# Grouped attention scores as full-array products over stacked query halves, with the convolution branch moved last

## The chip, the cores and the metric

One core of one Trainium2 chip runs the whole program. The metric is the device time of one execution in microseconds (us); the kernel before takes 743.72 us in the median of three runs (743.72 to 745.99).

## What is computed

The reference is a two-layer decoder trunk for 256 tokens of width 1024, in float32. Each layer mixes three branches that read one input projection, and then runs a gated feed-forward network with a short convolution:

```
h = rms_norm(x, attn_norm[l])
parts = split(h @ w_in[l])            # 13 parts
y_a = conv_module(...)                # 256 channels: 31 taps, layer norm, silu, 256x256 product
y_b = nsa_mixer(...)                  # 8 heads of 64 in 2 groups: compressed, selected, window attention
y_c = dilated_mixer(...)              # 3 dilations x 4 heads of 64
x = x + concat([y_a, y_b, y_c]) @ w_out[l]
x = x + conv_ffn(rms_norm(x, ffn_norm[l]), ...)   # up to 2 x 2816, 3 taps, silu * value, down
```

In `nsa_mixer` a head's query meets three sets of keys: its group's selected keys (256 tokens; with this sequence every block is selected), its window keys (256) and 15 compressed keys (padded to 16). Each set has its own softmax, and the three results are added with a gate each.

## The kernel before

Tokens lie in two tiles of 128 (`t`). Every dense product is made exact enough from two float32r halves of each operand: the weights come from memory as float32 (`raw`), ScalarE copies them to `whi` (L212) and VectorE subtracts to get `wlo` (L215), and `dense3` (L453 to L456) issues three products, hi by hi, hi by lo and lo by hi. Weights are consumed in one fixed stream of pieces, and `take` lets conversion run three pieces ahead.

The mixing stage of a layer runs from the chunks `a0`/`a` (keys, values, gates), `b` (queries of the grouped attention), `c0`/`c1` (convolution input) through a list of steps, `ORDER`: `np(i)` scores, softmax and transposes of head pair i of the grouped attention (`nsa_pair`), `nf(g)` its compressed branch and the products with the values (`nsa_finish`), `dq`, `dk`, `dv` dilated projections, `da`, `ds`, `pv` dilated attention, `t(n)` n taps of the convolution on VectorE, `ct` the convolution's tail (`conv_tail`: layer norm, silu, 256x256 product). Then `proj("out", ...)` sums eight pieces of 128 input rows, in `OUT_ORDER` (0 and 1 are the convolution's channels, 2 to 5 the grouped heads, 6 and 7 the dilated pairs): the first four pieces by piece, the last four (`TAIL`) for each quarter of the output. The steps are written in this order, and a planner orders each engine's instructions by the order written, their dependencies and costs that it assumes, so that work of neighbouring steps interleaves; each engine then runs its own list in order.

Grouped scores: q is turned (L703) into `QT`, 128 rows for a pair of heads, head j in rows 64j to 64j+63. `KG[g]` holds the keys of a group twice, in both row halves, as [window tile 1 ... compressed ... selected], 528 columns. A pair has three groups of scores: one for token tile 0 (L742, 272 columns: one key tile of each set and the compressed keys) and two for tile 1 (L756, 256 and 272 columns). In each group a float32 product for head 0 uses rows 0 to 63 of the array and one for head 1 rows 64 to 127; each stands in the trace as two matmul records. The scores lie in one PSUM tile of two banks (`sc_bank`, one buffer); VectorE adds the masks and takes the row minimum (L746, L759), ScalarE takes the exponential (L767, L771) and multiplies by the inverse sums (copies with a scale, L212 `ms<-ms,dd`), the array turns them (L783, L789), and L819 and L822 multiply with the values, head j into rows 64j of the PSUM tile `o`.

Compressed branch: `cs` is turned into `pc`, 64 rows, and one float32 product with 64 contraction rows (L823) adds both heads of a pair through `vbig`.

The end: `proj("down", ...)` sums 22 pieces into two single-bank tiles (`da`, token tile 0) and the two banks of one tile `db` (token tile 1). After all of them four adds to x are written, and in the last layer four stores.

PSUM tiles: `mm` three banks, `tp` two, `sc` two as one tile, `o` one. `conv_tail` uses `o` four times, and the out projection's last quarter uses `o` too.

Of the kernel before, what the change touches and what calls it, by code (L numbers as in the profile page):

```python
# [44 lines left out]
OUT_ORDER = (2, 3, 4, 5, 6, 0, 1, 7)  # L45
# [118 lines left out]
ORDER = "np(0) dq(0) t(6) np(1) dk(0) t(6) nf(0) np(2) dv(0) t(6) np(3) nf(1) da(0) dq(1) t(10) dk(1) t(100) ds(1) dv(1) ct(0) pv(1)"  # L164
# [26 lines left out]
def tile_hybrid_trunk(ctx, tc, x_in, pos_in, stream, feats, gains, norms, const_in, out):  # L191
# [261 lines left out]
    def dense3(o, a_hi, a_lo, b_hi, b_lo, start, stop):  # L453
        nc.tensor.matmul(o, a_hi, b_hi, start=start, stop=False)  # L454
        nc.tensor.matmul(o, a_hi, b_lo, start=False, stop=False)  # L455
        nc.tensor.matmul(o, a_lo, b_hi, start=False, stop=stop)  # L456
# [50 lines left out]
    for l in range(L):  # L507
# [87 lines left out]
        state["w1"] = lambda h: mp.tile([P, 3, 3, P], F32, tag="pT", name=f"w1{h}", bufs=4).rearrange("p a b c -> p (a b c)")[:, :PIECE]  # L595
# [4 lines left out]
        KG = [mp.tile([P, 528], F32, name=f"KG{g}") for g in range(2)]  # L600
# [3 lines left out]
        vbig = mp.tile([64, 2, 4, 64], F32, name="vbig")  # L604
# [7 lines left out]
        def section_a(split):  # L612
# [12 lines left out]
            for t in range(NT):  # L625
                kr = krs[t]
                tp = tp_bank(f"tpk{t}")
                for i in range(4):
                    nc.tensor.transpose(tp[:, i * P:(i + 1) * P], kr[:, i * P:(i + 1) * P], ident)
                for g in range(2):  # L630
                    copy_act(KG[g][:, P - t * P:2 * P - t * P], tp[:, g * P:(g + 1) * P])
                    copy_act(KG[g][:, 272 + t * P:272 + t * P + P], tp[:, (2 + g) * P:(3 + g) * P])

        def section_a0(split):
# [46 lines left out]
            for g in range(2):  # L681
                tt(vbig[:, g], cp2[0:64, 64 + g * 64:128 + g * 64].unsqueeze(1).broadcast_to([64, 4, 64]),
# [3 lines left out]
            for g in range(2):  # L686
                copy_act(KG[g][:, 256:272], tpq[:, g * 16:g * 16 + 16])

# [8 lines left out]
        QT = mp.tile([P, 4, S], F32, tag="QT", name="QT", bufs=1)  # L697
        banks = tok_chunk("b", 512, False, f"B{l}")
        qrs = rope(banks, 8, 0, (0, 1), "q")
        for t in range(NT):  # L700
            tp = tp_bank(f"tpq{t}")
            for i in range(4):
                nc.tensor.transpose(tp[:, i * P:(i + 1) * P], qrs[t][:, i * P:(i + 1) * P], ident)  # L703
            copy_act(QT[:, :, t * P:(t + 1) * P], tp.rearrange("p (k c) -> p k c", k=4))
# [10 lines left out]
        ts(dwh, dw, 0.5, None, ALU.mult)  # L715
# [14 lines left out]
        def nsa_pair(pair):  # L730
# [9 lines left out]
                for j in range(2):  # L740
                    hp_ = slice(j * 64, j * 64 + 64)
# [339 lines left out]
```

## Time and profile before

| | |
|---|---|
| median of 3 runs | 743.72 us |
| the profiled execution | 750.38 us, of it span 748.6 us |
| TensorE matmul (PE) busy | 729.1 us (97%) |
| VectorE (DVE) busy | 593.9 us (79%) |
| ScalarE (ACT) busy | 485.3 us (65%) |
| GpSimd (POOL) busy | 25.4 us (3%) |
| granted TensorE clock, mean | 0.993 |

A row of a timeline gives start, duration, engine, line, operation, what it writes and reads, shapes, and how many instructions are merged into it. Matmul durations include the way through the array, so consecutive ones overlap; what one costs is the distance from its start to the next start. A group's row gives count, busy time together, mean of one, and the idle time before it. "128*64" on a matmul means 128 contraction rows and 64 output rows of the array.

### The profile page before, as it was taken

To read this page: it belongs to the slowest core of one execution; us is meant where nothing else is said; L and a number is where in the kernel's file an instruction comes from. 1 tells how busy PE (TensorE), PEld (TensorE's weight loads), DVE (VectorE), ACT (ScalarE), POOL (GpSimd) and SP (SyncE) were. 2 spreads that over 40 slices of the span, in tenths; PEclk is the share of its full clock that TensorE was granted. 3 is DMA by queue.
4 is the path that set the end of the run, shared out by engine and by line. 5 is a ranking of instruction groups with operands and counts; after the bars stand their busy time and mean duration, and the time that the engine had idled before them with its cause. 6 is when DMAs were issued, how large, how long until landed. Compare 5 with 4: busy or idle time off the path is not lost.

```text
span 748.6 us, 13381 instructions
## 1 busy us (share of the span) xinstructions
PE 729.1 (97%) x4794; PEld 639.7 (85%) x4794; DVE 593.9 (79%) x1363; ACT 485.3 (65%) x1168; POOL 25.4 (3%) x67
## 2 busy tenths in 40 slices
PE   7899999999999999999999999999999999999997
PEld 5779777887899999988868887779779999999885
DVE  7689999986888888864487599999868988988441
ACT  5667999665577666653357579997546767676330
POOL 5200000000000000000040000000000000000000
PEclk9799999999999999999999999999999999999999
DMA  8654223453375665566538232236344666666631
GB/s 312 218 171 125 85 86 106 133 171 119 123 245 181 191 188 185 182 212 197 177 116 276 84 119 65 85 102 180 112 136 170 198 200 194 195 199 195 199 114 57
DMA packets 36005, 119.84 MB, mean 160 GB/s; under 512 B 4113, under 2 KB 4385, under 8 KB 35938
## 3 DMA queue, kind: packets, MB, share of 16 engines
q1 hardware_dynamic: 35714, 118.70, 50.1%
q8 instruction: 38, 0.62, 0.3%
q0 software_dynamic: 224, 0.28, 0.2%
q14 instruction: 29, 0.24, 0.1%
HBM read 117.91 MB, written 1.05 MB: 159 GB/s over the span
## 4 chain that ended last, share of the span: by engine, by line
PE 84%; DVE 7%; ACT 6%; issue 2%; DMA 1%; SPq 0%; DVEq 0%; ACTq 0%
PE up L455 10%; PE up L456 10%; PE up L454 10%; PE da L455 3%; PE da L454 3%; PE da L456 3%; PE db L454 2%; PE db L455 2%; PE db L456 2%; DVE wlo L215 2%; ACT whi L212 2%; PE hid L662 1%; PE sc L756 1%; PE Dk L454 1%; PE Dk L456 1%
## 5 line engine op out<-in xcount | busy, mean ns | idle before, releaser
L215 DVE TENSOR_TENSOR wlo<-raw,whi 128x1024 fp32r<-128x1024 f32 (+3 forms) x232 | 259.4, 1124 | 85.7 <-ACT whi L212 84.6
L212 ACT ACTIVATE whi<-raw 128x1024 fp32r<-128x1024 f32 (+3 forms) x232 | 224.6, 979 | 101.4 <-PE db L456 53.6
L454 PE MATMUL up<-xT_hi,whi 128*128 128x256 f32 x640 | 178.4, 279 | 0.0
L455 PE MATMUL up<-xT_lo,whi 128*128 128x256 f32 x640 | 178.2, 279 | 0.0
L456 PE MATMUL up<-xT_hi,wlo 128*128 128x256 f32 x640 | 178.2, 279 | 0.0
L455 PEld LDWEIGHTS up<-xT_lo,whi 128*128 128x128 f32 x640 | 121.5, 190 | 0.0
L454 PEld LDWEIGHTS up<-xT_hi,whi 128*128 128x128 f32 x640 | 120.1, 188 | 0.0
L456 PEld LDWEIGHTS up<-xT_hi,wlo 128*128 128x128 f32 x640 | 120.1, 188 | 0.0
L225 DVE SCALAR_TENSOR_TENSOR u<-up,ffeat,u 128x255 f32<-128x255 f32 (+1 forms) x176 | 80.0, 478 | 2.6
L225 DVE SCALAR_TENSOR_TENSOR acc<-a_pad,dwh,acc 128x256 f32<-128x256 f32 x120 | 53.6, 479 | 0.3 <-ACT acc L720 0.2
L1034 ACT ACTIVATE sl<-u 128x256 f32<-128x256 f32 x44 | 18.1, 416 | 48.7 <-DVE u L225 48.6
L1027 ACT ACTIVATE u<-up,ffeat 128x256 f32<-128x256 f32 x88 | 44.1, 551 | 0.0
L454 PE MATMUL da<-whi,gT_hi 128*128 128x512 f32 x88 | 34.3, 389 | 0.0
L455 PE MATMUL da<-wlo,gT_hi 128*128 128x512 f32 x88 | 34.3, 389 | 0.0
L456 PE MATMUL db<-whi,gT_lo 128*128 128x512 f32 x88 | 34.2, 389 | 0.0
L456 PE MATMUL da<-whi,gT_lo 128*128 128x512 f32 x88 | 34.2, 389 | 0.0
L454 PE MATMUL db<-whi,gT_hi 128*128 128x512 f32 x88 | 34.2, 389 | 0.0
L455 PE MATMUL db<-wlo,gT_hi 128*128 128x512 f32 x88 | 34.2, 389 | 0.0
L454 PE MATMUL A<-whi,xT_hi 128*128 128x280 f32 (+1 forms) x64 | 23.9, 373 | 0.4 <-ACT xT_hi L212 0.4
L212 ACT ACTIVATE ms<-ms,dd 128x128 f32<-128x128 f32 (+1 forms) x64 | 24.2, 448 | 0.0
L456 PE MATMUL A<-whi,xT_lo 128*128 128x280 f32 (+1 forms) x64 | 23.7, 372 | 0.4 <-DVE xT_lo L215 0.4
L455 PE MATMUL A<-wlo,xT_hi 128*128 128x280 f32 (+1 forms) x64 | 23.0, 363 | 0.0
(342 smaller groups left out, 1564.4 us busy)
## 6 DMA issues: line engine op xcount, KB each, us to landing
raw<-in_stream SPq DMA_DIRECT2D x172, 512.0 KB, 4.1
raw<-in_stream SPq DMA_DIRECT2D x48, 384.0 KB, 3.1
raw<-in_stream SPq DMA_DIRECT2D x8, 280.0 KB, 5.0
w<-in_stream SPq DMA_DIRECT2D x4, 512.0 KB, 6.1
gain<-in_norms SPq DMA_DIRECT2D x3, 512.0 KB, 3.5
x<-in_x SPq DMA_DIRECT2D x4, 256.0 KB, 4.3
out<-x SPq DMA_DIRECT2D x4, 256.0 KB, 2.1
feat<-in_feats SPq DMA_DIRECT2D x2, 339.0 KB, 5.1
```

Of the source, the lines that this page charges most:

```text
L212: return nc.scalar.activation(out=o, in_=i, func=AF.Copy, **kw)
L215: return nc.vector.tensor_tensor(out=o, in0=a, in1=b, op=op)
L225: return nc.vector.scalar_tensor_tensor(out=o, in0=a, scalar=s, in1=b, op0=op0, op1=op1)
L454: nc.tensor.matmul(o, a_hi, b_hi, start=start, stop=False)
L455: nc.tensor.matmul(o, a_hi, b_lo, start=False, stop=False)
L456: nc.tensor.matmul(o, a_lo, b_hi, start=False, stop=stop)
L662: nc.tensor.matmul(hp[:, 0:64], w1[i // 8][:, i % 8, :], flat[:, i].rearrange("p a h c -> p (a h c)"), start=(i == 0), stop=(i == 15))
L756: nc.tensor.matmul(sc[:, j * 512:j * 512 + n], QT[hp_, pair, P:2 * P], keys[hp_], start=True, stop=True)
L1027: nc.scalar.activation(out=u[:, h], in_=z, func=AF.Identity, scale=c[:, 2:3], bias=c[:, 3:4])
L1034: nc.scalar.activation(out=sl_, in_=u[:, 0], func=AF.Silu)
```

## The change

Keys and queries of the grouped attention are split into float32r halves. `zq` holds for each head the 64 high parts and the 64 low parts of q next to each other, so that one turn of 128 columns stacks them in the contraction rows (`QS`, 8 heads instead of 4 pairs: 16 turns a layer for 8). `KH` and `KL` take the place of `KG`; each score is the sum of two float32r products with all 128 rows, one with `KH` and one with `KL`. The scaling of the larger scores (128x256, 16 a layer) goes from ScalarE to VectorE. `pc` and `vbig` get 64 rows of zeros (GpSimd), and the compressed product becomes two with 128 contraction rows and 64 output rows. Fewer taps stand in the early steps, 16 of the 60 after `dv(1)`; `ct` comes after `pv(1)`, and the convolution's two pieces come last in the out projection, whose last quarter accumulates in `sc` instead of `o`. In the last layer the adds to x and the stores are written between the products of the down projection's tail, and the last quarter is made in two halves of 256 columns. The half of the taps' weights (`dwh`) is made on GpSimd. `pT` buffers shrink from nine blocks of 128 to eight.

```diff
-OUT_ORDER = (2, 3, 4, 5, 6, 0, 1, 7)
+OUT_ORDER = (2, 3, 4, 5, 6, 7, 0, 1)
...
-ORDER = "np(0) dq(0) t(6) np(1) dk(0) t(6) nf(0) np(2) dv(0) t(6) np(3) nf(1) da(0) dq(1) t(10) dk(1) t(100) ds(1) dv(1) ct(0) pv(1)"
+ORDER = "np(0) dq(0) t(3) np(1) dk(0) t(3) nf(0) np(2) dv(0) t(6) np(3) nf(1) da(0) dq(1) t(12) dk(1) t(20) ds(1) dv(1) t(100) pv(1) ct(0)"
...
-        KG = [mp.tile([P, 528], F32, name=f"KG{g}") for g in range(2)]
+        KH = mp.tile([P, 2, 528], F32R, name="KH")
+        KL = mp.tile([P, 2, 528], F32R, name="KL")
+
+        def split_keys(cols, src):
+            copy_act(KH[:, :, cols], src)
+            tt(KL[:, :, cols], src, KH[:, :, cols].bitcast(F32), ALU.subtract)
+
...
-        vbig = mp.tile([64, 2, 4, 64], F32, name="vbig")
+        vbig = sp.tile([P, D], F32, tag="xn", name=f"vbig{l}", bufs=1)[:, 0:512].rearrange("p (g r d) -> p g r d", g=2, r=4)
+        nc.gpsimd.memset(vbig[64:P], 0.0)
...
-                for g in range(2):
-                    copy_act(KG[g][:, P - t * P:2 * P - t * P], tp[:, g * P:(g + 1) * P])
-                    copy_act(KG[g][:, 272 + t * P:272 + t * P + P], tp[:, (2 + g) * P:(3 + g) * P])
+                tv = tp.rearrange("p (w g c) -> p w g c", w=2, g=2)
+                split_keys(slice(P - t * P, 2 * P - t * P), tv[:, 0])
+                split_keys(slice(272 + t * P, 272 + t * P + P), tv[:, 1])
...
-        QT = mp.tile([P, 4, S], F32, tag="QT", name="QT", bufs=1)
+        QS = mp.tile([P, 8, S], F32R, tag="QT", name="QS", bufs=1)
...
         for t in range(NT):
-            tp = tp_bank(f"tpq{t}")
-            for i in range(4):
-                nc.tensor.transpose(tp[:, i * P:(i + 1) * P], qrs[t][:, i * P:(i + 1) * P], ident)
-            copy_act(QT[:, :, t * P:(t + 1) * P], tp.rearrange("p (k c) -> p k c", k=4))
+            z = qrs[t].rearrange("p (h d) -> p h d", h=8)
+            zq = mp.tile([P, 8, P], F32, tag="pT", name=f"zq{t}", bufs=4).rearrange("p b c -> p (b c)")[:, 0:1024].bitcast(F32R)
+            zq = zq.rearrange("p (h u d) -> p h u d", h=8, u=2)
+            copy_act(zq[:, :, 0], z)
+            tt(zq[:, :, 1], z, zq[:, :, 0].bitcast(F32), ALU.subtract)
+            for half in range(2):
+                tp = tp_bank(f"tpq{t}{half}")
+                for i in range(4):
+                    nc.tensor.transpose(tp[:, i * P:(i + 1) * P], zq[:, half * 4 + i].rearrange("p u d -> p (u d)").bitcast(F32), ident)
+                copy_act(QS[:, half * 4:half * 4 + 4, t * P:(t + 1) * P], tp.rearrange("p (k c) -> p k c", k=4))
...
-        ts(dwh, dw, 0.5, None, ALU.mult)
+        ts(dwh, dw, 0.5, 1.0, ALU.mult, ALU.mult, eng=nc.gpsimd)
...
-                    hp_ = slice(j * 64, j * 64 + 64)
-                    nc.tensor.matmul(sc[:, j * 512:j * 512 + 272], QT[hp_, pair, 0:P], KG[g][hp_, P:P + 272], start=True, stop=True)
+                    for u, keys in enumerate((KH, KL)):
+                        nc.tensor.matmul(sc[:, j * 512:j * 512 + 272], QS[:, 2 * pair + j, 0:P], keys[:, g, P:P + 272], start=u == 0, stop=u == 1)
...
-                        hp_ = slice(j * 64, j * 64 + 64)
-                        nc.tensor.matmul(sc[:, j * 512:j * 512 + n], QT[hp_, pair, P:2 * P], keys[hp_], start=True, stop=True)
+                        for u, keys in enumerate((KH, KL)):
+                            nc.tensor.matmul(sc[:, j * 512:j * 512 + n], QS[:, 2 * pair + j, P:2 * P], keys[:, g, 256 * w:256 * w + n],
+                                             start=u == 0, stop=u == 1)
...
-                        copy_act(msl[j][:, w], msl[j][:, w], scale=dd[:, 1, j, w:w + 1])
+                        ts(msl[j][:, w], msl[j][:, w], dd[:, 1, j, w:w + 1], None, ALU.mult)
...
-            pc = mp.tile([P, S], F32, tag="cth", name=f"pc{g}", bufs=1)[0:64]
-            copy_act(pc, tp[0:64, 0:S])
+            pc = mp.tile([P, S], F32, tag="cth", name=f"pc{g}", bufs=1)
+            nc.gpsimd.memset(pc[64:P], 0.0)
+            copy_act(pc[0:64], tp[0:64, 0:S])
...
-                nc.tensor.matmul(ob[:, 0:S], vbig[:, g, 2 * pr:2 * pr + 2].rearrange("p a d -> p (a d)"), pc, start=False, stop=True, skip_group_check=True)
+                for j in range(2):
+                    nc.tensor.matmul(ob[j * 64:j * 64 + 64, 0:S], vbig[:, g, 2 * pr + j], pc, start=False, stop=True, skip_group_check=True)
...
-        def proj(name, npieces, kts, a_hi, a_lo, acc, tail):
-            def run(t, w, i, nhs=(0, 1)):
+        def proj(name, npieces, kts, a_hi, a_lo, acc, tail, done=None):
+            def run(t, w, i, nhs=(0, 1), part=None):
...
+                    c0, c1 = part or (0, 512)
+                    sl = slice(nh * 512 + c0, nh * 512 + c1)
+                    dense3(acc[t][nh][:, c0:c1], a_hi[:, kk, t * P:(t + 1) * P], a_lo[:, kk, t * P:(t + 1) * P], hi[:, sl], lo[:, sl],
+                           i == 0, i == npieces - 1, skip_group_check=done is not None and t == NT - 1 and nh == 1)
...
-                    for i in range(tail):
-                        run(t, ws[i], npieces - tail + i, (nh,))
+                    last = done is not None and t == NT - 1 and nh == 1
+                    for part in ((0, 256), (256, 512)) if last else ((0, 512),):
+                        for i in range(tail):
+                            run(t, ws[i], npieces - tail + i, (nh,), part)
+                        if done is not None:
+                            done(t, nh, part)
...
-        obs = [[mm_bank(f"oa{l}{i}") for i in range(2)], [mm_bank(f"ob{l}0"), o_bank(f"ob{l}1")]]
+        obs = [[mm_bank(f"oa{l}{i}") for i in range(2)], [mm_bank(f"ob{l}0"), sc_bank(f"ob{l}1")[:, 0:512]]]
...
+        dacc = [dnb, [scb[:, 0:512], scb[:, 512:1024]]]
+
+        def residual(t, nh, part):
+            sl = slice(nh * 512 + part[0], nh * 512 + part[1])
+            tt(x_sb[t][:, sl], x_sb[t][:, sl], dacc[t][nh][:, part[0]:part[1]], ALU.add)
+            if l == L - 1:
+                nc.sync.dma_start(out[0, t * P:(t + 1) * P, sl], x_sb[t][:, sl])
+
+        proj("down", NF, list(range(NF)), gT_hi, gT_lo, dacc, 4, residual if l == L - 1 else None)
```

## Rows read from the trace of the kernel before

**Rows 1.** The page, part 1: busy time, share, instructions of each engine.
```profile
PE 729.1 (97%) x4794; PEld 639.7 (85%) x4794; DVE 593.9 (79%) x1363; ACT 485.3 (65%) x1168; POOL 25.4 (3%) x67
```
**Rows 2.** By stretch: length, then busy PE, PEld, DVE, ACT, POOL, clock, DMA.
```profile
40.00:187.00 147.00, 145.70 (x892) 118.90 (x891) 130.71 (x399) 111.57 (x372) 0.00 (x0) 1.00 0.39 124
165.00:187.00 22.00, 21.84 (x132) 17.05 (x130) 15.37 (x32) 12.72 (x24) 0.00 (x0) 1.00 0.30 98
400.00:560.00 160.00, 156.77 (x966) 128.12 (x965) 134.79 (x412) 118.40 (x380) 0.00 (x0) 1.00 0.40 123
```
**Rows 3.** Timeline of PE from 467 to 472 us, around two groups of scores.
```profile
467.56 0.70 PE L756 MATMUL sc<-KG,QT 64*128 64x256 f32 x2
468.18 0.44 PE L789 MATMUL tp<-ident,ms 128*128 128x128 f32 x2
...
470.16 0.34 PE L455 MATMUL Dv<-wlo,xT_hi 128*128 128x384 f32 x1
470.33 0.33 PE L454 MATMUL Dv<-whi,xT_hi 128*128 128x384 f32 x1
470.59 0.73 PE L756 MATMUL sc<-KG,QT 64*128 64x272 f32 x4
471.25 0.45 PE L455 MATMUL Dv<-wlo,xT_hi 128*128 128x384 f32 x1
471.54 0.34 PE L456 MATMUL Dv<-whi,xT_lo 128*128 128x384 f32 x1
```
**Rows 4.** Timeline of PE near 20 us: dense float32r products of 280 columns.
```profile
19.98 0.29 PE L454 MATMUL A<-whi,xT_hi 128*128 128x280 f32 x1
20.11 0.29 PE L455 MATMUL A<-wlo,xT_hi 128*128 128x280 f32 x1
```
**Rows 5.** Timeline of PE near 484 us: values, compressed product, turns.
```profile
484.14 0.60 PE L819 MATMUL o<-pT,vN 128*64 128x256 f32 x4
484.57 0.39 PE L822 MATMUL o<-pT,vN 128*64 128x128 f32 x4
484.89 0.70 PE L823 MATMUL o<-pc,vbig 64*128 64x256 f32 x2
485.51 0.44 PE L789 MATMUL tp<-ident,ms 128*128 128x128 f32 x2
```
**Rows 6.** Timeline of PE near 441 us: the turns of q.
```profile
441.48 0.63 PE L703 MATMUL tpq<-ident,z1q 128*128 128x128 f32 x4 [0.71 <-DVE z1q L215]
441.86 0.42 PE L456 MATMUL Dq<-whi,xT_lo 128*128 128x384 f32 x1
```
**Rows 7.** Groups of DVE instructions from 60 to 190 us.
```profile
L225 DVE SCALAR_TENSOR_TENSOR acc<-a_pad,dwh,acc 128x256 f32<-128x256 f32 x60 | 26.8, 479 | 0.0
...
L220 DVE TENSOR_SCALAR dm<-dm,ddd 128x512 f32<-128x512 f32 x8 | 3.5, 481 | 0.0
...
L215 DVE TENSOR_TENSOR yT_lo<-o,yT_hi 128x256 fp32r<-128x256 f32 x4 | 1.7, 421 | 0.4 <-ACT yT_hi L212 0.4
...
L215 DVE TENSOR_TENSOR z1q<-z1q,rrq 128x512 f32<-128x512 f32 x2 | 1.3, 685 | 0.0
```
**Rows 8.** Groups of ACT instructions from 60 to 190 us.
```profile
L212 ACT ACTIVATE ms<-ms,dd 128x256 f32<-128x256 f32 x16 | 7.3, 502 | 0.0
```
**Rows 9.** Timeline of DVE: first and last step of the convolution's tail, layer 0.
```profile
158.81 0.41 DVE L215 TENSOR_TENSOR acc<-acc,lnm 128x256 f32<-128x256 f32 x1
...
175.24 0.43 DVE L215 TENSOR_TENSOR yT_lo<-acc,yT_hi 128x256 fp32r<-128x256 f32 x1 [0.92 <-ACT yT_hi L212]
```
**Rows 10.** The chain that ended last: the out projection's last add in layer 0.
```profile
192.39 0.68 DVE x L215
```
**Rows 11.** Timeline of the end, from 743 us.
```profile
743.16 0.39 PE L455 MATMUL db<-wlo,gT_hi 128*128 128x512 f32 x1
...
743.39 0.39 PE L456 MATMUL db<-whi,gT_lo 128*128 128x512 f32 x1
743.82 1.28 DVE L215 TENSOR_TENSOR x<-x,db 128x512 f32<-128x512 f32 x2 [4.75 <-PE db L456]
```

## What I expect and why

> **What bounds the kernel.** I read the page's busy times first, then busy time by stretch, then the timeline of PE, then groups of DVE and ACT. PE is busy 97% of the span, DVE 79%, ACT 65% [rows 1]. A busy PE need not be a full one, so the stretches count: in both mixing stages PE is busy 98 to 99%, at a granted clock of 1.00, the 2.4 GHz level [rows 2]. In the timeline the next matmul of a dense run starts 0.17 us after the last (384 columns) with nothing between [rows 3]. So PE's list of instructions sets the time, and what the change saves or adds is first the sum of starts-to-starts on PE. DVE comes second, and close: it is busy 130.7 of 147 us (89%) in the mixing stage of layer 0, 134.8 of 160 (84%) in layer 1 [rows 2]. That is the room in which DVE may take on work while PE's stage shrinks.
>
> **Part 1, scores.** From the code: 4 pairs, 3 groups each, 2 layers are 24 groups, each with two float32 products of two records. In the trace they come in two patterns. Where both heads stand next to each other (19 groups), the dense product before starts at 470.33 and would be followed 0.17 later; the group starts 0.09 after that, takes 0.66 to the next start, and that next dense product takes 0.29 instead of 0.17 [rows 3]: 0.09 + 0.66 + 0.12 = 0.87 us. Where other instructions came between the heads (5 groups), one head alone takes 0.62 [rows 3]; with the same 0.09 on entry, 1.42 us for two. Old sum: 19 x 0.87 + 5 x 1.42 = 23.6 us. The new group has four float32r products in the full array, the shape of the dense ones. The nearest row, 280 columns, has 0.13 us from start to start [rows 4]; by columns 0.126 for 272 and 0.119 for 256. New sum: 16 groups x 4 x 0.126 + 8 x 4 x 0.119 = 11.9 us. Saved: 11.7 us. Bounds: at the 0.17 of the 384-column products [rows 3] the new sum is 16.3 and 7.3 are saved; 12.5 if entry to the split groups cost more than I counted.
>
> The Trainium skill, TensorEngine Tiling (Array Packing), "Key Properties", says that a change of tiling mode drains the array; by that the 0.09 and 0.12 at the borders are part of the price and go, as I count them. The Trainium skill, TensorEngine Tiling (Array Packing), "When to Use Tiling", speaks against the change: a contraction of 64 should be packed two to the array. The trace agrees that packing works (0.66 for two heads, 0.62 for one); what the rule would make of the time is a rival below.
>
> **Part 2, turns of q.** Eight more a layer. Four take 0.38 us from the first to the next dense start [rows 6]: 16 x 0.095 = 1.5 us, I take 1.6. The step before them now also has an ACT copy and a DVE subtraction of 128x512 (0.69 each by the nearest DVE row) [rows 7]; PE already waited 0.71 us there for the rotated q [rows 6], and I charge the longer chain below, in what PE doesn't realise; its bounds are nothing, if dense work of `dq` is moved in front, and 1.4 us a layer.
>
> **Part 3, compressed products.** One now takes 0.62 us plus 0.10 on entry: the four 128-column records before it, two at a time side by side, would be through at 484.79, and it starts at 484.89 [rows 5]. The new one has the shape of the product with the values, whose four records of 256 columns take 0.43 us [rows 5], with no change of shape before it and the 0.10 then on exit. 8 x (0.72 - 0.53) = 1.5 us saved; bounds zero (heads not side by side) and 2.3 (no exit).
>
> **PE together:** 11.7 + 1.5 - 1.6 = 11.6 us less, 5.8 a layer.
>
> **Part 4, what DVE takes on.** Per layer: 16 scalings of 128x256. The nearest row is the same operation on 128x512, 0.481 us [rows 7]; half is 0.24, the 128x256 subtraction from PSUM, 0.42, is the upper end; I take 0.27, nearer to the same operation, 4.3 us (3.8 to 6.7). Low parts of the keys: four of 128x256 from PSUM at 0.42 and one small, 1.9 us. Low parts of q: two of 128x512 at 0.685 [rows 7], 1.4 us. Together 7.6 us (7.1 to 10.0). `dwh` on GpSimd takes a little off DVE, and GpSimd is busy 25 us in all [rows 1]; the two clears of zeros wait in its queue for the buffers of `xn` and `cth`, and behind the first stand the rotation tables in layer 1, which I cost at nothing as long as the planner doesn't put the clear ahead of them; if it does, some 2 us. ACT loses 16 x 0.50 = 8 us a layer [rows 8] and gains four copies of q.
>
> Layer 0: 130.7 + 7.6 = 138.3 us of DVE in 147 - 5.8 = 141.2 us, 98%. Layer 1: 134.8 + 7.6 = 142.4 in 154.2, 92%. In layer 0 that is more than DVE can hold while its operands come from PE and ACT. At 95% the stretch takes 145.6 us and saves 1.4, at 97% 142.6 and 4.4; I take 3. In layer 1 I take 5 of 5.8, the rest going to the longer q chain. Realised: 8 us of 11.6.
>
> **Part 5, taps later, convolution last.** The early steps lose 6 taps, 6 x 0.45 = 2.7 us of DVE (26.8 us for 60) [rows 7] where scores wait for row minima, and 16 taps, 7.2 us, come after `dv(1)`, where DVE is at 15.4 of 22 us [rows 2]. I cost the move at nothing, covered by out-projection pieces that don't need the convolution: its tail ended at 175.7 [rows 9], the last add of the out projection came at 192.4 [rows 10], so PE had some 16 us of work behind it; 2 of 8 pieces (24 matmuls of 0.23 [rows 11], 5.5 us) need it and 5.8 are saved, which leaves 5 us by which it may slip. Without that cover it is the rival that is slower.
>
> **Part 6, the end.** Both adds to the last token tile ran after the last matmul, 1.28 us together [rows 11], though the first one's operands were complete 12 matmuls earlier: reads of one bank of the two-bank tile waited for the other. With the last quarter halved, one add of 128x256 (0.42) [rows 7] remains: 0.86 us saved at best. But a wait of that kind also works the other way: PE's next product into the tile, with the rest of the list behind it, waits for the add that was written before it. After the first quarter: 0.43 to the add's start, 0.69 for the add, less the 0.23 pitch, about 0.9 us; after the first half 0.6 to 0.7. I take both, as the nearest row has it: 1.6 - 0.9 = 0.7 us lost; bounds 0.9 gained and 0.8 lost.
>
> The Trainium skill, PSUM — Partial Sum Buffer, "Terms", says that TensorE writing and VectorE reading one bank at once is an error; by that the halves of one bank must take turns, and at least the second hold stands. Were only that one real, the end would cost about nothing.
>
> **Sum.** 3 + 5 - 0.7 = 7.3 us. Profiled execution: span 748.6 to 741.3, execution 750.4 to 743.1; it was 6.7 above the median, with no clock loss to explain it, so I take the difference off the median: 743.7 - 7.3 = **736.4 us**. A difference of 0.3%, 2.2 us, is about what a measurement of this kernel can tell from none.
>
> **Rivals.**
> *All of PE's saving is realised*, DVE at 98% in layer 0 holds and the end gains: 743.7 - 11.6 - 0.9 = 731.2. For it: taps can fill any gap of DVE, and ACT is relieved. Against it: DVE at 89% now.
> *DVE becomes the bound* and gets no further than 92%: layer 0 takes 138.3 / 0.92 = 150.3 us, 3.3 more than now, layer 1 154.8, 5.2 less; with the end 742.5. For it: the DVE sum above. Against it: DVE's present gaps are partly waits for PE.
> *The convolution's tail is exposed.* The tail takes 16.9 us from its first subtraction to its last [rows 9]. If the 16 taps and the 7.6 us of new DVE work aren't absorbed, it ends 14.8 us later in its layer, 9.8 beyond the 5 us of cover, and PE stops in front of the convolution's pieces in both layers: 743.7 + 19.6 - 11.6 + 0.7 = 752.4. It decides from a slip of 5 us.
> *The new products are no faster than the old records.* If each of 96 took the 0.31 us of one old record (0.62 for two) [rows 3], scores cost 29.8, 6.2 more than now, and the time is 743.7 + 6.2 + 0.1 + 0.7 = 750.7. The 0.13 of rows 4 speaks against it. The advice on packing in the Trainium skill, TensorEngine Tiling (Array Packing), "When to Use Tiling", would lead here.
>
> **Chances.** Forecast 0.47 (733 to 740), full saving 0.20, DVE the bound 0.18, exposed tail 0.11, no faster products 0.04. Faster by over 0.3% (below 741.5): 0.47 + 0.20 + under half of DVE's case, 0.75. Within: the rest of that case, 0.10. Slower: 0.15. The range goes from 730.5, past the full saving, to 745, past the DVE case; outside it are the exposed tail, the slow products and a few hundredths below.
>
> **What would show it.** Scores as four 128-row records of about 0.12 us from start to start, about 12 us in all; DVE at 93 to 97% in layer 0's mixing stage; PE gaps there that end with DVE, at the q turns above all; in the last 4 us two gaps of PE of 0.6 to 0.9 us that end with adds. A gap of PE of several us in front of the out projection's last pieces would make the forecast wrong upward; none at all, with DVE at 98%, downward.

## The result, and the profile after

| | before | after |
|---|---|---|
| median, same chip | 744.86 us (743.72 to 749.9, 4 runs) | 754.94 us (753.24 to 758.48, 4 runs) |
| ratio of the times | 1 | 1.0119, 95% interval 1.0073 to 1.0164 |
| the profiled execution | 750.38 us, span 748.6 | 754.79 us, span 753.0 |
| mean granted TensorE clock | 0.993 | 0.986 |

The change makes the kernel some 9 to 10 us slower (1.2%); I had forecast 7.3 us faster, in a range that ends at 745.0. The page's first part for after, beside [rows 1]: PE is busy 11 us less and DVE 13 us more, near the 11.6 and 15.2 of the forecast, and the span is longer all the same.

```profile
PE 718.1 (95%) x4838; PEld 642.3 (85%) x4838; DVE 606.7 (81%) x1408; ACT 476.3 (63%) x1134; POOL 28.7 (4%) x75
```

The same by stretch, as in [rows 2] (length, busy PE, PEld, DVE, ACT, POOL, clock, DMA):

```profile
165.00:187.00 22.00, 19.82 (x110) 15.34 (x108) 18.59 (x49) 12.34 (x23) 0.00 (x0) 1.00 0.58 196
548.00:555.00 7.00, 5.98 (x15) 4.27 (x14) 2.38 (x5) 1.45 (x4) 0.00 (x0) 0.52 0.17 66
561.90:565.30 3.40, 3.40 (x17) 3.26 (x16) 1.69 (x5) 2.41 (x6) 0.00 (x0) 0.50 0.02 5
189.80:193.20 3.40, 3.40 (x17) 3.27 (x17) 2.03 (x7) 2.26 (x6) 0.00 (x0) 0.51 0.02 5
40.00:187.00 147.00, 143.96 (x920) 123.62 (x918) 138.23 (x427) 107.71 (x357) 0.62 (x2) 1.00 0.42 132
400.00:560.00 160.00, 148.49 (x942) 126.33 (x940) 134.95 (x418) 109.26 (x351) 0.61 (x2) 0.98 0.37 115
```

DVE is busy 138.23 of 147 us in layer 0, and 18.59 of the 22 us from 165 to 187, where it had 15.37. (The windows are the same, but the mixing stage of after began 1.8 us earlier in layer 0 and 5.7 us earlier in layer 1, so they don't hold quite the same work.) PE in layer 1 falls to 148.49 of 160. Three stretches stand at the lower clock level, about 0.5; the kernel before had none between its start and its end.

The scores in the timeline of PE, to be set beside [rows 3]: four records of 0.12 to 0.13 us from start to start, 0.50 for a group of 272 columns, and the next dense product follows without a pause.

```profile
458.22 0.33 PE L455 MATMUL Dv<-wlo,xT_hi 128*128 128x384 f32 x1
458.39 0.29 PE L754 MATMUL sc<-KH,QS 128*128 128x272 f32 x1
458.51 0.29 PE L754 MATMUL sc<-KL,QS 128*128 128x272 f32 x1
458.64 0.29 PE L754 MATMUL sc<-KH,QS 128*128 128x272 f32 x1
458.76 0.29 PE L754 MATMUL sc<-KL,QS 128*128 128x272 f32 x1
458.89 0.34 PE L456 MATMUL Dv<-whi,xT_lo 128*128 128x384 f32 x1
```

The compressed product and the turns of q, beside [rows 5] and [rows 6]:

```profile
440.54 1.06 PE L715 MATMUL tpq<-ident,zq 128*128 128x128 f32 x8 [0.86 <-DVE zq L215]
441.36 0.42 PE L455 MATMUL Dk<-wlo,xT_hi 128*128 128x384 f32 x1
...
480.04 0.60 PE L837 MATMUL o<-pc,vbig 128*64 128x256 f32 x4
480.57 0.55 PE L801 MATMUL tp<-ident,ms 128*128 128x128 f32 x3
```

DVE's groups from 40 to 187 us, beside [rows 7]: the taps, the new scaling, the new low parts of keys and q.

```profile
L225 DVE SCALAR_TENSOR_TENSOR acc<-a_pad,dwh,acc 128x256 f32<-128x256 f32 x60 | 27.6, 484 | 0.1
...
L220 DVE TENSOR_SCALAR ms<-ms,dd 128x256 f32<-128x256 f32 x16 | 5.0, 349 | 0.0
...
L215 DVE TENSOR_TENSOR KL<-tpk,KH 128x256 fp32r<-128x256 f32 x4 | 1.6, 417 | 0.1
...
L215 DVE TENSOR_TENSOR zq<-z1q,zq 128x512 fp32r<-128x512 f32 x2 | 1.3, 694 | 0.0
```

What PE waited for, from the view of waits (total us, times, longest). In the kernel before, the longest such line past its start-up is 1.2 (`tpq`), and the first two of these are 0.2 and 0.9:

```profile
PE tpxf L359 <- DVE xnf L225: 5.8, 2, 2.9
...
PE up L1029 <- ACT uts L212: 3.4, 2, 1.8
PE pwp L869 <- DVE acc L225: 2.8, 1, 2.8
...
PE oa L454 <- ACT yT_hi L212: 2.2, 2, 1.2
...
PE db L454 <- DVE x L215: 1.3, 2, 0.8
```

And the place of the loss, PE at the end of layer 1's mixing stage (the bracket is idle time and what ended it):

```profile
543.75 0.47 PE L456 MATMUL ob<-whi,yT_lo 128*128 128x512 f32 x1
547.05 2.60 PE L869 MATMUL pwp<-acc,feat 128*128 128x256 f32 x8 [2.82 <-DVE acc L225]
...
550.68 0.79 PE L454 MATMUL oa<-whi,yT_hi 128*128 128x512 f32 x1 [1.02 <-ACT yT_hi L212]
...
558.07 0.39 PE L456 MATMUL ob<-whi,yT_lo 128*128 128x512 f32 x1
561.38 1.78 PE L359 MATMUL tpxf<-ident,xnf 128*128 128x128 f32 x8 [2.92 <-DVE xnf L225]
```

PE stops for the convolution's tail (`pwp`, then `oa`), then for the norm that the next stage needs (`tpxf`), and after each stop part of what follows runs at half clock: behind the row at 550.68 a record of 512 columns takes 0.43 us from start to start (the next ones begin at 551.27, 551.70, 552.12), later 0.23.

**One measure for all runs.** Executions of one kernel scatter by some 10 us, and what the traces show of the causes lies outside the mixing stages (last section). So each run below also has the length of its two mixing stages: from the first record of `b` (`B` in the timeline of PE) to the first record of `up` (the turns of its head), both layers added. It comes from one traced execution each, so it has no interval; e12 and e18 are the same kernel and give 327.1 and 327.3. The wait of `up` comes just after the end of this measure. Before: 206.0 - 44.0 = 162.0 and 573.4 - 402.5 = 170.9, together 332.9 us. After: 161.5 + 179.1 = 340.6. So 7.7 us of the loss lie there, where 11.6 were to be saved on PE; layer 0 gained 0.5, layer 1 lost 8.2.

### The profile page after: what moved, and what is told of

It reads as the page before. It is cut to its first block, busy times and chain, and to the rows that moved or that the text cites. A ratio compares the mean times of both kernels' runs of the same rounds, so it can differ in the third digit from the quotient of the medians.

```text
span 753.0 us, 13469 instructions
## 1 busy us (share of the span) xinstructions
PE 718.1 (95%) x4838; PEld 642.3 (85%) x4838; DVE 606.7 (81%) x1408; ACT 476.3 (63%) x1134; POOL 28.7 (4%) x75
## 4 chain that ended last, share of the span: by engine, by line
PE 77%; DVE 8%; ACT 7%; DMA 4%; issue 2%; POOL 0%; SPq 0%; ACTq 0%; DVEq 0%
PE up L455 10%; PE up L454 10%; PE up L456 10%; DMA raw<-in_stream 3%; PE da L454 3%; PE da L455 3%; PE da L456 3%; PE db L454 3%; DVE wlo L215 3%; PE db L455 2%; PE db L456 2%; ACT whi L212 2%; PE hid L669 1%; PE dsc L909 1%; PE Dk L456 1%
## 5 line engine op out<-in xcount | busy, mean ns | idle before, releaser
L454 PE MATMUL db<-whi,gT_hi 128*128 128x512 f32 (+1 forms) x92 | 35.2, 382 | 1.3 <-DVE x L215 1.3
L455 PE MATMUL db<-wlo,gT_hi 128*128 128x512 f32 (+1 forms) x92 | 35.0, 380 | 0.0
L456 PE MATMUL db<-whi,gT_lo 128*128 128x512 f32 (+1 forms) x92 | 35.0, 380 | 0.0
L454 PE MATMUL Dv<-whi,xT_hi 128*128 128x384 f32 x64 | 22.2, 347 | 0.1
```

Source lines behind the costliest of these rows:

```text
L454: nc.tensor.matmul(o, a_hi, b_hi, start=start, stop=False, **kw)
L455: nc.tensor.matmul(o, a_hi, b_lo, start=False, stop=False, **kw)
L456: nc.tensor.matmul(o, a_lo, b_hi, start=False, stop=stop, **kw)
```

## The experiments

Runs were taken on several chips, each beside the kernel before: where chips differ, compare the ratios.

| run | what it is | median, us | ratio to before, 95% | mixing stages, us |
|---|---|---|---|---|
| | before | 744.9 to 748.2 | 1 | 332.9 |
| | after | 754.9 | 1.0119 (1.0073 to 1.0164) | 340.6 |
| e2 | after, old order | 760.6 | 1.0189 (1.0147 to 1.0231) | 344.4 |
| e3 | before, new order | 747.8 | 1.0005 (0.9971 to 1.0039) | 333.3 |
| e4 | after, late sums | 754.5 | 1.0107 (1.0074 to 1.0139) | 341.5 |
| e5 | after, old order, late sums | 758.5 | 1.0158 (1.0105 to 1.0212) | 345.5 |
| e6 | after, scaling on ACT | 747.7 | 1.0026 (0.9992 to 1.0061) | 334.5 |
| e7 | e6, old order, late sums | 752.6 | 1.0103 (1.0067 to 1.0139) | 338.0 |
| e8 | before, scaling on DVE | 752.9 | 1.0114 (1.0064 to 1.0164) | 340.3 |
| e9 | after, old scores, keys and q | 751.7 | 1.0057 (1.0020 to 1.0093) | 338.3 |
| e10 | before, 20 of 60 taps | 752.6 | 1.0074 (1.0037 to 1.0110) | 335.3 |
| e11 | after, 20 of 60 taps | 743.6 | 0.9937 (0.9890 to 0.9983) | 326.1 |
| e12 | after, scaling on POOL | 742.8 | 0.9938 (0.9897 to 0.9980) | 327.1 |
| e14 | e6, low parts of q on POOL | 757.5 | 1.0150 (1.0055 to 1.0246) | 342.3 |
| e15 | before, scaling on POOL | 749.3 | 1.0022 (0.9988 to 1.0056) | 334.3 |
| e16 | e12, late sums | 740.7 | 0.9930 (0.9888 to 0.9972) | 327.7 |
| e17 | e12, old order | 741.8 | 0.9954 (0.9918 to 0.9990) | 329.5 |
| e18 | e12 again | 739.3 | 0.9908 (0.9875 to 0.9942) | 327.3 |

**Is it the order?** Theory A: the convolution's tail, now last, is exposed. Theory B: DVE's new work makes it the bound. Theory C: the early sums hold PE. The edit of e2 is the first below; e3 makes the opposite one to the kernel before (with the out projection's last quarter in `sc`, as in after), e4 the second, with the adds and stores written behind all products again, e5 both.

```
-OUT_ORDER = (2, 3, 4, 5, 6, 7, 0, 1)
+OUT_ORDER = (2, 3, 4, 5, 6, 0, 1, 7)
-ORDER = "... t(3) ... t(3) ... t(12) dk(1) t(20) ds(1) dv(1) t(100) pv(1) ct(0)"
+ORDER = "... t(6) ... t(6) ... t(10) dk(1) t(100) ds(1) dv(1) ct(0) pv(1)"

-proj("down", ..., dacc, 4, residual if l == L - 1 else None)
+proj("down", ..., dacc, 4, None)
```

> The changed kernel with the two order lines of before put back (taps all before ds(1), conv_tail before pv(1), conv pieces fifth to seventh in the out projection); all else as changed. Theory A (the convolution's tail, put last, is exposed, and the out projection has nothing left beside it and beside the norm that follows): about 737 us, 6 to 9 below before, no stretch at half clock after 40 us, no wait of pwp above 1 us. Theory B (the 7.6 us a layer of new DVE work bind): 745 to 752, since that work stays. Theory C (the holds in the last layer's end cost the time): 753 or so, hardly moved.

> The kernel before with only the order of the change: ORDER, OUT_ORDER, and the out projection's last quarter in sc. Theory A: 752 to 758 us, 8 to 13 above before, with a wait of PE in front of the convolution's pieces in both layers and a stretch at half clock there. Theory B: within 2 us of before, since no DVE work is added. Theory C: within 2 us of before.

> The changed kernel with the last layer's adds and stores written after all products again, last quarter whole. Theory A: within 1 us of the changed kernel (754 to 756): the two holds go (1.6 us) and the two adds of 0.69 come back behind the last matmul (1.5 us). Theory C: 750 or less.

> Both undone: old order and late sums; what remains is scores, zero rows, scaling on DVE, dwh on GpSimd. Theory A: within 1 us of the run with the old order alone, about 737 us. Theory B: 745 to 752.

Theory A falls twice: after with the old order is some 5 us slower still, and the new order costs the kernel before nothing (mixing stages 333.3). Theory C falls: without the early sums the time is the same (754.5 against 754.9). None of the three had 760.6 or 758.5 for e2 and e5: theory B, with 745 to 752, was too low as well. With the old order the backlog of DVE shows up earlier, in front of the dilated rotation (waits of PE in e2):

```profile
PE tpxf L359 <- DVE xnf L225: 3.8, 4, 2.1
PE tpdk L886 <- DVE z1dk L215: 3.6, 1, 3.6
...
PE lnm L844 <- DVE acc L225: 2.5, 1, 2.5
```

**Is it the scaling or the split?** Rival D: the split itself costs, by the chain of keys and q. e6 is after with the line below; e7 is e6 with the edits of e5; e8 makes the opposite edit to the kernel before, and nothing else; e9 is after with scores, keys and q as before.

```
-ts(msl[j][:, w], msl[j][:, w], dd[:, 1, j, w:w + 1], None, ALU.mult)
+copy_act(msl[j][:, w], msl[j][:, w], scale=dd[:, 1, j, w:w + 1])
```

> After, with one line taken back: the sixteen scalings of 128x256 score tiles per layer are on ACT again. Theory B (the DVE work that the change adds is what costs; it fills the slips in which the convolution's taps ran, so that the conv tail and the norm chain come late): 16 x 0.349 = 5.6 us a layer leave DVE, most of what was added; ACT takes back 16 x 0.50 = 8.0. Time 738 to 747, that is at or below the kernel before; the waits of the residual transposes (tpxf) and of up at the end of the attention become shorter than 2 us each, and the half-clock stretches of 13.6 us shrink. Rival D (not the scaling but the split itself: the subtractions for keys and q ahead of the scores, or the order of the fillers that shorter scores leave): 752 to 757, as after.

> After, with the scaling on ACT, the order of before and the sums after all products: what is left of the change is the scores in the full array with their split keys and stacked q, and the zero-row compressed products. Theory B: against the run with old order and late sums and the scaling on DVE (758.45) it gains 8 to 18 us and comes to 738 to 748, since 2.9 us a layer of DVE are left of 8 added, and PE has 5.8 us a layer less to do. Rival D: 753 to 758.

> Before, with one line changed: the sixteen scalings per layer of the 128x256 score tiles on DVE and not on ACT. Products, order and sums as before. Theory B: 5.6 us a layer are added to a DVE that is busy 131 of 147 us; with no shorter products beside it the time rises by 4 to 12 us over the kernel before, to 749 to 757, with half-clock stretches that the kernel before doesn't have. Rival D: the scaling is hidden or even helps ACT, within 2 us of the kernel before.

> After, with the scores, keys and q as before (row pairs in full fp32, no subtractions for keys and q, no stacked q turns); the scaling stays on DVE, the zero rows, the order and the early sums stay. It tells the split from the scaling. Theory B with the scaling as the main part: PE gets 5 us a layer of work back but waited for that time anyway, DVE loses 2.9 us a layer: 748 to 756, within 4 us of after. If the split of keys and q were the cause (Rival D): 742 to 747, as before. If the shorter scores were a real gain in after that only the scaling hid: above 758.

One line decides: put back, it gives some 7 us (ratios of 1.0107 and 1.0119 against 1.0026); added to the kernel before, it costs 6 us in the medians, 8.5 by the ratio, and 7.4 us of the mixing stages (340.3 against 332.9), with products, written order and sums of before. e8 has the same stops at `tpxf` and `up` as after (first fence), where the kernel before has 0.2 and 0.9; in e6 (second) they are 0.3 and 0.9. Rival D isn't excluded as a smaller part: e9, with the old scores and the scaling still on DVE, is at 1.0057 against 1.0107 and 1.0119, so as long as DVE has the scaling the new scores bring no gain and perhaps a loss (the intervals overlap).

```profile
PE tpxf L359 <- DVE xnf L225: 5.6, 2, 3.2
...
PE up L1010 <- ACT uts L212: 3.1, 2, 1.6
```
```profile
PE tpxf L359 <- DVE xnf L225: 0.3, 1, 0.3
```

Every run with the scaling on DVE and all taps (after, e2, e4, e5, e8, e9) has them, 3.5 to 5.8 us for `tpxf` and 2.9 to 3.4 for `up`; no other run has over 0.5 and 0.9. How it reaches the norm, 100 us after the scaling, stands in e8's timeline of DVE, layer 0, from the out projection's adds to the normed row:

```profile
182.70 1.40 DVE L215 TENSOR_TENSOR x<-x,oa 128x512 f32<-128x512 f32 x2
184.07 1.23 DVE L215 TENSOR_TENSOR sp<-raw,sp 128x1024 fp32r<-128x1024 f32 x1
...
187.23 1.22 DVE L215 TENSOR_TENSOR wlo<-raw,whi 128x1024 fp32r<-128x1024 f32 x1
...
189.63 1.42 DVE L225 SCALAR_TENSOR_TENSOR xnf<-x,nrf,gain 128x512 f32<-128x512 f32 x2
```

Conversions of weights (`sp`, `wlo`) stand between the adds and inside the norm's chain of steps of some 0.2 us; the one at 187.23 alone holds the next step until 188.36. PE's last product of the out projection started at 187.74, and PE then idled 2.40 us:

```profile
190.53 1.34 PE L359 MATMUL tpxf<-ident,xnf 128*128 128x128 f32 x8 [2.40 <-DVE xnf L225]
```

The same stretch can be measured in every run: from the start of the last `oa` product, which the chain waits for, to the end of the normed row. Its two ends in the kernel before, layer 0, from the timelines of PE and DVE (the row of DVE holds two steps, the second ends at 192.48):

```profile
186.32 0.39 PE L456 MATMUL oa<-whi,yT_lo 128*128 128x512 f32 x1
...
191.06 1.42 DVE L225 SCALAR_TENSOR_TENSOR xnf<-x,nrf,gain 128x512 f32<-128x512 f32 x2
```

In every run without these stops it takes 6.15 to 6.16 us, in both layers, and 23 or 24 `ob` products (5.2 to 5.4 us) stand behind that `oa` product to cover it. In e8 it takes 8.07 and 8.88 us, with 21 products behind it; in e9 7.63 with 19; in e2 and e5 7.2 to 7.6 with 20 to 22. In after (and in e4) it is mostly the cover that is gone: the chain takes 6.63 and 6.66 us, but the out projection's products that need no convolution had been drawn forward into PE's gaps, so that only some 24 were left after the late tail, and 12 of them, 2.7 us, behind the last `oa` (layer 1 in the rows above, from 555.33 to 558.07).

One reservation: the planner orders the lists anew for every edit. By their starts, some 300 of the 1363 instructions of DVE apart from the scalings stand in another order in e8 than in the kernel before (some 180 in e15, below, whose time is that of before). No run holds the order fixed, so the runs show what the line costs through this planner; how much of it is DVE's lateness and how much the other order is not shown.

The expectations for e8 (749 to 757) and e9 (748 to 756) held, e6 came out just above its 738 to 747, and e7's did not hold (738 to 748): with the scaling on ACT, the old order and the late sums together still cost some 5 us.

**Where does PE's saving go?** In e6 the time is that of the kernel before, and nothing of the 11.6 us that I took off PE shows. e10 and e11 take DVE's load away on both sides (40 of the 60 taps of a layer are not computed), e12 puts the scaling on POOL, e14 is e6 with the subtraction of q on POOL.

```
-taps = [(b, k) for k in range(1, TAPS) for b in range(2)]
+taps = [(b, k) for k in range(1, 11) for b in range(2)]

+ts(msl[j][:, w], msl[j][:, w], dd[:, 1, j, w:w + 1], 1.0, ALU.mult, ALU.mult, eng=nc.gpsimd)

-tt(zq[:, :, 1], z, zq[:, :, 0].bitcast(F32), ALU.subtract)
+nc.gpsimd.tensor_tensor(out=zq[:, :, 1], in0=z, in1=zq[:, :, 0].bitcast(F32), op=ALU.subtract)
```

> Before, with 40 of the 60 DVE taps of each layer left out (taps 11 to 30 of the convolution are not computed): 40 x 0.48 = 19 us a layer leave DVE and nothing else changes. It is the base line for the next run. Where DVE is not the bound of the kernel before, 742 to 747, within 4 us of it; where it is already the bound in the attention part, down to 735.

> After, with the same 40 taps of each layer left out: DVE has 11 us a layer less to do than in the kernel before, in spite of all that the change adds to it. Theory B (DVE is what the gain of the products was lost to): now the 5.8 us a layer of PE come through, and the run is 8 to 12 us faster than before with few taps, at 728 to 737. Rival G (the gain is lost to something else: the weight stream's landing, ACT, the order that PE's fillers take, the half clock): the difference to before with few taps stays under 4 us, or has the other sign as with all taps (+9).

> After, with the sixteen scalings of 128x256 tiles per layer on POOL, which is 4% busy: DVE loses 5.6 us a layer and ACT doesn't get it back, so it is the cheapest relief that there is, if POOL is fast enough. Theory B: 740 to 748, like the run with the scaling on ACT (747.7) or below it by up to 5. If one scaling takes POOL over 1 us, the turns behind it wait for it, 4 x 4 times a layer: 750 to 757.

> After with the scaling on ACT, and the two subtractions of q (2 x 0.69 us a layer) on POOL: DVE has 1.4 us a layer less. Theory B: 744 to 748, up to 3 us below the run with the scaling on ACT alone (747.7). If POOL needs much longer than 0.7 us for 128x512, the stacked turns of q wait for it and the time is 748 to 752.

With few taps, after is 9.0 us faster than before in the medians and 9.3 in the mixing stages: the difference is inside the 8 to 12 us of theory B, and rival G falls, though e11's 743.6 itself lies above the 728 to 737 expected. But e10 alone missed: it is slower than before by 5 to 6 us, though 19 us of DVE a layer are gone. Its stage of layer 0 is 3 us longer (165.0), with no wait of over 0.9 us in it. I take the planner's new order as the likely cause, not shown. So a part of the 9 us may be e10's own loss: against the kernel before with all its taps, e11 is 0.6% faster and its mixing stages are 6.9 us shorter. e14 missed as well: the subtraction takes POOL 1.90 us where DVE took 0.69, and the turns of q wait for it in both layers.

```profile
L711 POOL TENSOR_TENSOR zq<-z1q,zq 128x512 fp32r<-128x512 f32 x2 | 3.8, 1904 | 0.1
```
```profile
PE tpq L715 <- POOL zq L711: 4.8, 2, 2.5
```

**The control.** e12 was faster than before, but it also relieves ACT, by 8 us a layer. Rival H: that is the whole gain. e15 moves only the scaling of the kernel before to POOL; e16, e17 and e18 are e12 with late sums, with the old order, and unchanged.

> Before, with only the sixteen scalings per layer moved from ACT to POOL (0.80 us each there, 0.50 on ACT): ACT has 8 us a layer less, DVE and PE the same. Theory B (before is bound by PE, the new products shorten PE, and what was lost was DVE's): 743 to 748, as before, since ACT was hidden. The run of after with the scaling on POOL is then 3 to 8 us faster than this one, and that is what the products are worth. Rival H (ACT's 8 us a layer are what the version with POOL gains, and the split brings nothing): this run is at 740 to 744, within 2 us of it.

> After with the scaling on POOL and the last sums behind all products, as in the kernel before. The two holds at the end (0.8 and 0.5 us in the waits) go, the tail from the last product to the end grows from 3.8 to 5.2 us: within 1 us of the same kernel with early sums, 741 to 745. A gain or loss of over 2 us would say that the early sums matter after all.

> After with the scaling on POOL and the order of before (taps early, convolution tail before the last pair, its rows sixth and seventh of the out projection). With the scaling on DVE the old order was 5 us slower than the new, with it on ACT also about 5. Theory B: DVE's backlog of early taps stands in front of the dilated rope in this order, so 745 to 750. If the order doesn't matter once the scaling is off DVE and ACT: 741 to 745.

> The kernel after with the scaling on POOL once more, beside the three others on the same chip: 740 to 745, as in its first run (742.8), and below the kernel before.

Rival H falls: relief of ACT gives the kernel before nothing (1.0022). With the scaling on POOL on both sides, what is left of the change (scores, compressed products, order, early sums together) is worth 1.0022 - 0.9908 = 1.1%, 8.5 us, with an interval of 5 to 12 (half-widths of 0.0034, added in squares), and 334.3 - 327.3 = 7.0 us in the mixing stages. e18 beats both kernels, by 0.9% and about 2%; the intervals of e16, e17 and e18 overlap, so neither the early sums nor the order makes a clear difference there (e17's mixing stages are 2.2 us longer). Theory B had expected 745 to 750 for e17 and missed. POOL's group of scalings and the stretches of e18:

```profile
L222 POOL TENSOR_SCALAR ms<-ms,dd 128x256 f32<-128x256 f32 x16 | 13.1, 833 | 30.2 <-DVE negm L758 11.1 <-ACT whi L212 8.8 <-ACT cs L812 6.7
```
```profile
40.00:187.00 147.00, 144.72 (x921) 124.19 (x920) 135.66 (x415) 108.08 (x357) 13.71 (x18) 1.00 0.43 128
400.00:560.00 160.00, 155.93 (x1027) 133.90 (x1026) 139.29 (x418) 114.96 (x361) 11.90 (x18) 1.00 0.36 110
```

DVE is still busy 92% in layer 0, yet PE's wait on POOL's scaled tiles is only 0.8 us in all. The Trainium skill, Perfetto Trace Analysis, "Optimizing Scalar/DVE Operations", says that with a saturated DVE it may pay to move work to ScalarE or even GpSimd, and doubts the latter, as the two share a read port. Of that the runs bear out the first half (754.9, then 747.7 and 739.3 to 742.8); of the doubt they show little: taps take 490 ns in e18 against 478 in e6, 0.7 us for all sixty, and that the port is the reason is not shown.

**Settled and open.** Settled: that one line on DVE costs 6 to 8.5 us, with stops of PE at the end of the mixing stage; with that work on an idle engine the rest of the change gains about 8.5 us. Open: how much of the stops is load and how much the planner's order; why e10 is slower than before; why the scaling on ACT (e6) gives only half of what POOL gives. Of the 7.1 us between the mixing stages of e6 and e18, PE's waits on ACT from 60 to 575 us are 2.8 (5.6 against 2.8), and the score products, which in e6 often have turns and waits between them, take 16.8 us from start to start against 13.2; the two overlap in part.

## Why the prediction was wrong, point by point

**What bounds the kernel.** Right that PE sets the time and DVE comes second and close. But the busy share that I read off [rows 2] doesn't tell when DVE starts to hold others up. Counted over layer 0's mixing stage (from `B` to `up`), DVE is busy 88% in the kernel before (143.2 of 162.0 us), 89% in e8 (147.3 of 165.3), 92% in after (148.9 of 161.5) and 92% in e18 (145.5 of 158.7): the second and the third have the stops, the first and the last don't.

**Part 1, scores**: right in its mechanism, about 1 us too good. The row has 0.50 us a group, and beside dense products the borders of 0.09 and 0.12 are gone. But over all 24 groups the starts-to-starts add up to 13.0 us (forecast 11.9): 13 of the 96 records, most of them next to turns or value products, take 0.20 to 0.29. The turns use the full array too, so the border's price isn't one of the tiling mode alone. The advice to pack a contraction of 64 two to the array (the Trainium skill, TensorEngine Tiling (Array Packing), "When to Use Tiling") didn't lead here: a packed pair took 0.66 us [rows 3], the four full ones take 0.50. **Part 2**: turns of q cost 1.9 us more by the same count (forecast 1.6). **Part 3**: 0.53 us in the row and in three others, as forecast, 0.58 in the four that follow a dense product. By these counts PE's saving was some 1.6 us smaller than the 11.6; by its busy time in the mixing stages it was 8.2 in e18 (319.8 us against 328.0). **Part 6**: PE's two holds are there, 0.78 and 0.51 us; the last layer's down projection is 2.1 us longer, the tail after its last product 1.4 shorter (749.25 to 753.0, against 743.39 to 748.6): 0.7 lost, as I had it.

```profile
747.36 0.42 DVE L215 TENSOR_TENSOR x<-x,db 128x256 f32<-128x256 f32 x1 [1.78 <-PE db L456]
...
747.83 0.39 PE L454 MATMUL db<-whi,gT_hi 128*128 128x256 f32 x1 [0.51 <-DVE x L215]
...
749.25 0.28 PE L456 MATMUL db<-whi,gT_lo 128*128 128x256 f32 x1
749.57 0.42 DVE L215 TENSOR_TENSOR x<-x,db 128x256 f32<-128x256 f32 x1 [1.79 <-PE db L456]
```

**Part 4 is the step that failed**, and not in its sum. I added 7.6 us to DVE's 130.7 and wrote 138.3; the trace has 138.23 in that window. So close a hit is partly luck: the scaling was undersized (0.35 us each and not 0.27, though the operations overlap and are busy 5.0 us for sixteen), and from `B` to `up` the stage has only 5.7 us more of DVE (148.9 against 143.2). What failed is the next sentence, the turn from a busy share into time: at 94 to 97% I let 8 of PE's 11.6 us come through, as if DVE's work could fill any gap. Measured, the mixing stages are 7.7 us longer. The runs show another price. The dependent chains on DVE (the convolution's norm, the row norm) stand in one list with taps and conversions of weights, and slip by whole steps of 0.5 and 1.2 us; PE's cover is shorter than the chain, and then PE stops at the end of the stage, in both layers. In e8 a lone 4.7 us a layer on DVE cost 3.2 and 4.2 us of the two stages (165.3 against 162.0, 175.1 against 170.9), with no other line edited.

**Part 5** was wrong in its cover. 5 us of slip were to be hidden; counted from the start of the stage, the products of the convolution (`pwp`) started 9.5 us later than in the kernel before in layer 0 (134.8 against 125.3) and 18.1 in layer 1 (150.2 against 132.2), and what I had counted as cover, the out projection's other products, had been drawn forward. The move itself costs nothing, as I said: in e3 they start at 125.4 and 132.4. The slip comes with the new work.

**Sum.** I found no clock loss in the traced execution of the kernel before, which was 6.7 us above the median. There is one: its granted clock up to `B` is 0.88, which goes with a `B` some 4 us later than at 1.00, and its layer 0 had the slower pace of the last section. Taking the difference off the median was right all the same.

**Rivals.** "The convolution's tail is exposed" named 752.4 and had 0.11. Its sign came, PE's gap of 2.8 us in front of `pwp` in layer 1, and its time was near the result (10 us above before instead of 8.7), but that is luck: it had new work and move together as the cause, with 19.6 us of exposure, while the larger stop is the one at `tpxf`, and with the tail in its old place the loss is there too (e2, e8). "DVE becomes the bound" had the engine, but priced it by a share of 92% and came to 742.5, since it left out the stops and the clock. I read no row for what PE does after it has stopped for several us. With the scaling off DVE and ACT the gain is of the forecast's size: e18 is 0.9%, 7 us, below the kernel before, and some 8.5 below e15, where 7.3 were forecast.

## What to carry to other kernels

When work moves onto an engine that is busy near 90% of a stage, don't price it by the share that results: look for the chains on that engine that another engine waits for at the end of the stage, and count what stands between their steps and what work the waiting engine has left to cover them. Before giving elementwise work to the second-busiest engine, look at the one that is idle: 0.83 us on POOL, for which PE waited 0.8 us in all, was better than 0.35 on DVE. What PE waits for soon must not go there (1.90 us for the low part of q cost 9 to 10 us in all, e14 against e6). To find which part of a large change costs, put each part alone onto the kernel before; here one line alone reproduced a loss of that size (1.0114 against 1.0119).

## What the runs showed of the hardware that was not expected

**The clock after a stop.** After PE idled 2.9 us for `tpxf`, what followed ran at 0.50 to 0.51, and after the stops around `pwp` at 0.52 (rows above), 13.6 us in all in after; e8 has two such stretches after its two stops for `tpxf`, e6 and e18 none between start and end. As the same products take 0.43 us there and 0.23 later, a stop costs more than its length.

**Two paces of the same products.** The up projection runs dense at full clock, and yet in one of two paces, each kept for a whole layer: 851 or 884 products in 100 us, 117.8 or 113.3 ns each, some 4.2 us a layer. Layers 0 and 1 of the kernel before, then of e3:

```profile
210.00:310.00 100.00, 100.00 (x851) 100.00 (x851) 33.48 (x74) 17.09 (x34) 1.00 0.63 194
580.00:680.00 100.00, 100.00 (x884) 100.00 (x884) 33.44 (x73) 18.76 (x38) 1.00 0.63 195
```
```profile
210.00:310.00 100.00, 100.00 (x884) 100.00 (x884) 35.60 (x79) 18.16 (x37) 1.00 0.65 201
580.00:680.00 100.00, 100.00 (x851) 100.00 (x851) 32.47 (x71) 17.43 (x35) 1.00 0.64 190
```

**The start.** `B` begins anywhere from 39.7 to 44.4 us, and in the 18 traced executions that goes with the granted clock up to there: 39.7 to 40.2 us in the seven with 1.00, 41.9 to 42.5 in the seven with 0.92, 44.0 to 44.4 in the four with 0.88, whatever the kernel. e12 and e18, the same kernel, differ in a third place: e12 waited 1.5 and 1.7 us for DVE near 380 us and then ran at half clock, and needed 196.8 us from `up` of layer 0 to the next `B`, against 191.8.

Start and pace together come to some 13 us, as much as the scatter from 741 to 753 us in runs of the kernel before; only one of these was traced, so that they are the cause there is likely and not shown. What sets the pace stayed open. The comparison by the mixing stages is free of both.
